# GpSimd's two-input work on VectorE and ScalarE, and the prompt's probability-value products by pairs of heads

## The chip, the cores and the metric

One Trainium2 chip, and one of its cores: TensorE (PE, with its weight loads shown apart as PEld), VectorE (DVE), ScalarE (ACT), GpSimd (POOL) and the queue engine SP, which issues most of the loads. The metric is the time of one execution on the device in microseconds (us). Before the change three runs gave a median of 1501.34 us (1498.47 to 1504.32).

## The reference

One step of a two-layer decoder over a prompt of 512 rows and a sample group of 8 sequences of 8 rows. In each layer a normalised input goes through one projection, whose columns feed a pooling mixer, a state-space mixer (causal convolution, SiLU, scan in chunks of 128) and multi-head latent attention; the three results go through an output projection and a residual add, and an MLP with a squared ReLU follows. Cut to what the change touches:

```python
def mixer(h, p, pos0, pool_hist, conv_hist, ssm_h0, attend):
    u, z, xbc, dt_raw, cq, ckv, kpe = split_in_proj(h @ p['w_in'])
    pool_out, new_pool = pool_mix(u, pool_hist, pos, p['pool_w'], p['pool_scale'])
    ssd_out, new_conv, new_ssm = ssd_mix(z, xbc, dt_raw, conv_hist, ssm_h0, p)
    mla_out, ckv_n, kpe_r = mla_mix(cq, ckv, kpe, pos, p, attend)
    y = jnp.concatenate([pool_out, ssd_out.astype(h.dtype), mla_out], axis=-1) @ p['w_out']

# ssd_mix: the convolution's output and the gate z go through SiLU
    xbc, new_conv = causal_dwconv(xbc, conv_hist, p['conv_w'], p['conv_b'])
    xbc = jax.nn.silu(xbc.astype(jnp.float32))

# mla_prompt_attn, for each block of 128 queries, all 6 heads
        sc = jnp.where(kpos[None, :] <= qpos[:, None], sc, -jnp.inf)
        pr = jax.nn.softmax(sc, axis=-1).astype(ckv.dtype)
        return jnp.einsum('bhts,bsc->bthc', pr, ckv)
```

## The kernel before

The rows are cut into two chunks: chunk 0 holds 256 rows of the prompt, chunk 1 the other 256 and the 64 sample rows. Activations lie with features on the partitions and rows along the free axis. Every large product is made from two roundings of each operand, a high and a low part: `wblock` (L183) loads half a weight block of 128 x 512 (`wr`), ACT makes its high part `wh` (L191), and the low part `wl = wr - wh` is a subtraction of two SBUF operands (L192). L192 goes to DVE for the MLP's weights and for the second half of each block of the other projections, and to POOL for the first half and for `w_uq`. `gemm` (L196) then issues three matmuls a k-tile (L201 to L203).

In a layer, `mixer` runs for each chunk: `w_in` (L502) goes through 14 column tiles, and `evac` (L460) takes each result from PSUM. The tiles named xb go through `conv_tile` (L387): two or three DVE steps bring them into `XB`, POOL copies three old columns to its front (L391), DVE makes four taps (L400, L402), ACT a sigmoid (L413 to L415), and POOL the product with it (L405, L407). There is one buffer for `XB`. The z tiles get the same sigmoid and a product on POOL (L479). The tiles cq0 and cq1 become `qhl`, from which `mla_proj` (L522) makes the queries `qT`.

`prompt_attn` (L558) goes through pairs of heads j, the two heads hh of a pair, and two blocks of 128 queries b. With `nb` blocks of 128 keys (1 or 2 in chunk 0, 3 or 4 in chunk 1) it makes scores (L570 to L574), their maximum (DVE, L576), exponentials with a sum (ACT, L579), a reciprocal (DVE, L580), the scaling by it (POOL, L581), `nb` transposes (L584), their copy `pT` to SBUF (L587 on ACT, L589 on DVE) and `nb` products with the values (L591), which write 64 partitions of PSUM: head hh = 0 the lower, hh = 1 the upper half. An fp32 product shows as two matmul records. `sample_attn` (L597) does the same for the samples from paged keys and values; POOL takes part in it at L671 and L698. `pr` and `pT` have two buffers each, shared by both.

What runs side by side is set by `Weave` (L272): generators of instructions that are taken in turn by what they have spent. The products of the MLP (`ffn`, L995) fill the time beside attention and scan. A scheduler of the compiler then sets the final order of each engine's instructions; on the chip each engine takes its own in that order.

## Time and profile before

| | us |
|---|---|
| median of three runs | 1501.34 |
| the profiled execution's own time | 1500.04 |
| its span in the profile | 1498.2 |
| PE busy | 1418.7 (95%) |
| DVE busy | 1067.8 (71%) |
| ACT busy | 816.9 (55%) |
| POOL busy | 341.5 (23%) |

The profiled execution lies 1.8 us above its span and 1.3 us under the median. Engines work beside each other, so the shares don't add up. PE shows the largest share, but matmuls are pipelined and their records overlap; how long a product holds PE is read from the distance of one start to the next.

### The profile page before, as it was taken

The page shows a single profiled execution, that of the slowest core. Times are in us where ns is not written, and L with a number is a line of the kernel's source. Part 1 is how long each engine was busy: PE and PEld are TensorE (multiplying, and loading weights), DVE is VectorE, ACT ScalarE, POOL GpSimd, SP SyncE. Part 2 cuts the span into 40 slices and gives each one's busy share as a digit, 9 for nine tenths or more (in the row PEclk, how much of TensorE's full clock was granted, in tenths as well). Part 3 has the DMA queues.
Part 4 walks back from the last instruction along what each step waited for, and adds up shares of the span by engine and source line. Part 5 has one row for each costly group of instructions (what it writes and reads, how often), then busy time and mean ns, then how long its engine had stood idle before and what let it go on. Part 6 is the DMA issues. An engine that isn't in the chain of part 4 may idle for free.

```text
span 1498.2 us, 30372 instructions
## 1 busy us (share of the span) xinstructions
PE 1418.7 (95%) x10528; PEld 1355.6 (90%) x10528; DVE 1067.8 (71%) x2225; ACT 816.9 (55%) x1717; POOL 341.5 (23%) x458
## 2 busy tenths in 40 slices
PE   5988988999999979999999999999999999999997
PEld 4867977998999978999999998889989999999997
DVE  7878759776666779865566668976866667765765
ACT  6555636555565656655454556545656565443444
POOL 5456424222200235200100035511231011000000
PEclk8999999999999999999999999989999999999999
DMA  6322425667546634434554543455675455444443
GB/s 215 108 96 77 146 70 172 201 201 211 154 138 186 199 106 135 149 104 149 163 153 153 168 153 111 149 169 165 197 225 158 135 174 165 152 150 149 149 152 108
DMA packets 151995, 228.96 MB, mean 153 GB/s; under 512 B 17826, under 2 KB 60962, under 8 KB 151714
## 3 DMA queue, kind: packets, MB, share of 16 engines
q1 hardware_dynamic: 138178, 216.69, 46.3%
q10 hardware_dynamic: 13664, 10.34, 2.3%
q8 instruction: 83, 1.36, 0.4%
q14 instruction: 70, 0.57, 0.1%
HBM read 219.32 MB, written 7.64 MB: 151 GB/s over the span
## 4 chain that ended last, share of the span: by engine, by line
PE 81%; DVE 11%; issue 2%; DMA 2%; ACT 2%; SPq 1%; POOL 0%; ACTq 0%; DVEq 0%; POOLq 0%
PE dn L203 9%; PE dn L201 9%; PE dn L202 9%; PE up L203 9%; PE up L201 9%; PE up L202 9%; PE in L203 2%; PE in L202 2%; PE in L201 2%; PE out L201 2%; PE out L202 2%; PE out L203 2%; PE o L591 2%; DVE cv L402 2%; PE spo L717 1%
## 5 line engine op out<-in xcount | busy, mean ns | idle before, releaser
L201 PE MATMUL up<-gh_f,wh_up 128*128 128x256 f32 (+1 forms) x1024 | 308.7, 302 | 5.0 <-DVE UE L425 2.6
L203 PE MATMUL up<-gh_f,wl_up 128*128 128x256 f32 (+1 forms) x1024 | 307.2, 301 | 3.4 <-DVE wl_up L192 1.9
L202 PE MATMUL up<-gl_f,wh_up 128*128 128x256 f32 (+1 forms) x1024 | 306.9, 300 | 0.7 <-DVE gl_f L236 0.5
L201 PE MATMUL dn<-hh,wh_dn 128*128 128x256 f32 (+1 forms) x1024 | 303.8, 297 | 3.3 <-ACT wh_dn L191 3.2
L203 PE MATMUL dn<-hh,wl_dn 128*128 128x256 f32 (+1 forms) x1024 | 304.2, 297 | 0.0
L202 PE MATMUL dn<-hl,wh_dn 128*128 128x256 f32 (+1 forms) x1024 | 303.3, 297 | 0.0
L191 ACT ACTIVATE wh_dn<-wr_dn 128x512 fp32r<-128x512 f32 x256 | 160.9, 631 | 184.6 <-PE dn L202 126.1
L191 ACT ACTIVATE wh_up<-wr_up 128x512 fp32r<-128x512 f32 x256 | 160.3, 630 | 172.4 <-PE up L202 107.4
L192 DVE TENSOR_TENSOR wl_dn<-wr_dn,wh_dn 128x512 fp32r<-128x512 f32 x256 | 179.2, 701 | 84.1 <-ACT wh_dn L191 72.6
L192 DVE TENSOR_TENSOR wl_up<-wr_up,wh_up 128x512 fp32r<-128x512 f32 x256 | 182.2, 715 | 73.6 <-ACT wh_up L191 63.3
L201 PEld LDWEIGHTS up<-gh_f,wh_up 128*128 128x128 f32 x1024 | 195.4, 191 | 9.0 <-DVE UE L425 2.8
L203 PEld LDWEIGHTS up<-gh_f,wl_up 128*128 128x128 f32 x1024 | 195.2, 191 | 6.8 <-DVE wl_up L192 4.6
L202 PEld LDWEIGHTS up<-gl_f,wh_up 128*128 128x128 f32 x1024 | 195.7, 191 | 2.6 <-DVE gl_f L236 0.8
L201 PEld LDWEIGHTS dn<-hh,wh_dn 128*128 128x128 f32 x1024 | 193.3, 189 | 3.9 <-ACT wh_dn L191 3.7
L203 PEld LDWEIGHTS dn<-hh,wl_dn 128*128 128x128 f32 x1024 | 193.2, 189 | 1.4 <-issue 0.7
L202 PEld LDWEIGHTS dn<-hl,wh_dn 128*128 128x128 f32 x1024 | 193.3, 189 | 1.2 <-issue 0.9
L201 PE MATMUL in<-gh_h,wh_in 128*128 128x256 f32 (+3 forms) x448 | 137.9, 308 | 16.2 <-DVE cq L490 7.5
L203 PE MATMUL in<-gh_h,wl_in 128*128 128x256 f32 (+3 forms) x448 | 137.6, 307 | 3.5 <-DVE wl_in L192 2.4
L202 PE MATMUL in<-gl_h,wh_in 128*128 128x256 f32 (+3 forms) x448 | 137.2, 306 | 2.1 <-DVE gl_h L236 2.1
L192 POOL TENSOR_TENSOR wl_in<-wr_in,wh_in 128x512 fp32r<-128x512 f32 (+1 forms) x55 | 72.9, 1326 | 155.8 <-ACT wh_in L191 149.8
L192 POOL TENSOR_TENSOR wl_out<-wr_out,wh_out 128x512 fp32r<-128x512 f32 x32 | 41.8, 1306 | 278.7 <-ACT wh_out L191 278.7
L201 PEld LDWEIGHTS in<-gh_h,wh_in 128*128 128x128 f32 (+1 forms) x448 | 85.1, 190 | 18.9 <-issue 7.9
(349 smaller groups left out, 2849.4 us busy)
## 6 DMA issues: line engine op xcount, KB each, us to landing
wr_up<-in_w_up SPq DMA_DIRECT2D x256, 256.0 KB, 2.8
wr_dn<-in_w_down SPq DMA_DIRECT2D x256, 256.0 KB, 2.8
wr_in<-in_w_in SPq DMA_DIRECT2D x110, 256.0 KB, 2.8
wr_out<-in_w_out SPq DMA_DIRECT2D x64, 256.0 KB, 2.9
ku<-in_kcache SPq DMA_DIRECT2D x96, 128.0 KB, 2.9
nat<-in_ncache SPq DMA_DIRECT2D x96, 64.0 KB, 2.0
ku<-in_kcache ACTq DMA_DIRECT2D x32, 128.0 KB, 3.7
wr_uq<-in_w_uq SPq DMA_DIRECT2D x12, 256.0 KB, 2.8
```

Source lines behind the costliest of these rows:

```text
L191: A.activation(hh, r, AF.Copy)
L192: (V if eng == 'v' or (f and eng is None) else G).tensor_tensor(ll, r, hh.bitcast(F32), op=ALU.subtract)
L201: T.matmul(ps[:mw, :cw], wh[:, kk, :mw], ah, start=(k == 0), stop=False)
L202: T.matmul(ps[:mw, :cw], wh[:, kk, :mw], al, start=False, stop=False)
L203: T.matmul(ps[:mw, :cw], wl[:, kk, :mw], ah, start=False, stop=(k == nk - 1))
L402: V.scalar_tensor_tensor(cv[:, :n], X[:, k:k + n], par(l, 'conv_w', m * 4 + k), cv[:, :n], op0=ALU.mult, op1=ALU.add)
L591: mark_pe[f"pa{l}{c}"] = T.matmul(po[64 * hh:64 * hh + 64, b * P:b * P + P], vT[i // 2][:, i % 2, h * 64:h * 64 + 64], pT[:, i * P:i * P + ...
L717: mark_pe[f"s{l}{2 * pq_ + 1}"] = T.matmul(po[:, 64 * u:64 * u + NR], nat[:, g], pT[:, o_:o_ + NR], start=False, stop=True, skip_group_che ...
```

## The change

Four things, all in the code that is shown above.

- The tables of engines at L93: the products with the sigmoids (L405, L407, L479) and the correction of the rotary keys of the cache (L671) go from POOL to DVE.
- `wblock`: all subtractions L192 go to DVE.
- The scalings by the reciprocal, L581 in the prompt and L698 in the samples, become ACT activations with a scale of one value a partition.
- `prompt_attn`: the loops over heads and query blocks change places. For one query block the steps up to `pT` are made for both heads of a pair; then their products stand in turns, one of head 0, one of head 1. `pT` is copied by ACT for the second head and by DVE for the first, where it was by query block. The yields keep their sum, 1.1 nb a pair.

POOL keeps the memsets, the small copies, the squares at the start (L247 to L251), the pooling sums (L436), L886, L890 and two products at the end (L1021).

```diff
-    E_XA, E_Z, E_KR, E_PR = G, G, G, G
+    E_XA, E_Z, E_KR = V, V, V
...
-                (V if eng == 'v' or (f and eng is None) else G).tensor_tensor(ll, r, hh.bitcast(F32), op=ALU.subtract)
+                V.tensor_tensor(ll, r, hh.bitcast(F32), op=ALU.subtract)
...
                 po = psum('ac', f"o{l}{c}{j}")
-                for hh in range(2):
-                    h = 2 * j + hh
-                    for b in range(2):
-                        nb = 2 * c + b + 1
-                        nk = nb * P
+                for b in range(2):
+                    nb = 2 * c + b + 1
+                    nk = nb * P
+                    pTs = []
+                    for hh in range(2):
+                        h = 2 * j + hh
...
-                        E_PR.tensor_scalar(pr[:, :nk], pr[:, :nk], nm[:, 3:4], 1.0, op0=ALU.mult, op1=ALU.mult)
+                        A.activation(pr[:, :nk], pr[:, :nk], AF.Copy, scale=nm[:, 3:4])
...
-                        if b:
+                        if hh:
                             A.activation(pT[:, :nk], tp[:, :nk], AF.Copy)
                         else:
                             V.tensor_copy(pT[:, :nk], tp[:, :nk])
-                        for i in range(nb):
+                        pTs.append(pT)
+                        yield 0.4 * nb
+                    for i in range(nb):
+                        for hh in range(2):
+                            h = 2 * j + hh
                             mark_pe[f"pa{l}{c}"] = T.matmul(
                                 po[64 * hh:64 * hh + 64, b * P:b * P + P], vT[i // 2][:, i % 2, h * 64:h * 64 + 64],
-                                pT[:, i * P:i * P + P], start=(i == 0), stop=(i == nb - 1)).ins
-                        yield 0.55 * nb
+                                pTs[hh][:, i * P:i * P + P], start=(i == 0), stop=(i == nb - 1)).ins
+                    yield 0.3 * nb
...
-                G.tensor_scalar(prs[1], prs[1], nm[:, 1:2], 1.0, op0=ALU.mult, op1=ALU.mult)
+                A.activation(prs[1], prs[1], AF.Copy, scale=nm[:, 1:2])
```

The scheduler makes a new order of all engines from this. Five lines more in the file move the line numbers: L591 of before is L596 after.

On PE, in layer 0, chunk 1, the products of heads 4 and 5 with the first query block (`pT0140` is `pT` of layer 0, chunk 1, head 4, query block 0; `vT00` and `vT01` are the values of the chunks). Before:

```order
L202 MATMUL up0024_5980<-gl_f00_3370,wh_up0024_0_5970 128x256
L591 MATMUL o012_6101<-pT0140_6117,vT00_906 64x128 x2
L591 MATMUL o012_6101<-pT0140_6117,vT01_3498 64x128
L570 MATMUL sc0151_6678<-kT00_905,qT01_3074 128x256
L571 MATMUL sc0151_6678<-kT01_3497,qT01_3074 128x256
```

After:

```order
L733 MATMUL spv01_6294<-ol01_3756,uv0_200 64x64
L596 MATMUL o012_6101<-pT0140_6117,vT00_906 64x128
L596 MATMUL o012_6101<-pT0150_6247,vT00_906 64x128
L596 MATMUL o012_6101<-pT0140_6117,vT00_906 64x128
L596 MATMUL o012_6101<-pT0150_6247,vT00_906 64x128
L596 MATMUL o012_6101<-pT0140_6117,vT01_3498 64x128
L596 MATMUL o012_6101<-pT0150_6247,vT01_3498 64x128
L585 MATMUL pt0151_6647<-cst_77,pr0151_6643 128x128 x4
```

The three products of head 5 stood in a burst of their own 36 rows further on and now stand between those of head 4. Not all bursts are so clean: in most the scheduler puts the first product of one head ahead, alone, and the others follow in turns.

On DVE, shortly after the start (`r_q00` is the factor of the queries, `qT00` the queries of layer 0, chunk 0, `gl_h0_1` the low part of chunk 1's input, `sm00` small steps of the scan). Before:

```order
L236 SCALAR_TENSOR_TENSOR gl_h0_1_155<-x1_in_152,prm0_73,gh_h0_1_154 128x320
L499 SCALAR_TENSOR_TENSOR r_q00_306<-tab00_214,r_q00_306 128x256
L786 SCALAR_TENSOR_TENSOR sm00_435<-sm00_435 128x18
L192 TENSOR_TENSOR wl_in004_4_644<-wr_in004_4_641,wh_in004_4_643 128x512
L531 TENSOR_TENSOR qT00_590<-q000_597,r_q00_306 128x256
L531 TENSOR_TENSOR qT00_590<-q001_605,r_q00_306 128x256
```

After:

```order
L481 TENSOR_TENSOR ckvn00_217<-in001_483,r_in00_211 128x256
L499 SCALAR_TENSOR_TENSOR r_q00_306<-tab00_214,r_q00_306 128x256
L779 TENSOR_TENSOR sm00_435<-dt00_432,prm0_73 128x12
L531 TENSOR_TENSOR qT00_590<-q000_597,r_q00_306 128x256
L782 SCALAR_TENSOR_TENSOR sm00_435<-sm00_435 128x18
L531 TENSOR_TENSOR qT00_590<-q001_605,r_q00_306 128x256
L531 TENSOR_TENSOR qT00_590<-q002_619,r_q00_306 128x256
L531 TENSOR_TENSOR qT00_590<-q003_627,r_q00_306 128x256
L784 TENSOR_SCALAR sm00_435<-sm00_435 128x18
L793 TENSOR_SCALAR sm00_435<-sm00_435 128x18
L236 SCALAR_TENSOR_TENSOR gl_h0_1_155<-x1_in_152,prm0_73,gh_h0_1_154 128x320
```

The row of L236 in the first piece is the last of eight; all eight now stand behind `r_q` and four of the `qT`. On ACT the two steps of `r_q` (L217, L218) stood around chunk 1's high parts (L235) and now stand together, ahead of the two `kT` copies (L537, L538) and of L235.

On DVE, from one xb tile of chunk 1 to the next (`XB011` is tile 1; `wl_out` belongs to the output projection of chunk 0). Before:

```order
L390 TENSOR_TENSOR XB011_2164<-in017_2139,r_in01_1897 128x256
L394 TENSOR_TENSOR XB011_2164<-in017_2139,r_in01_1897 128x8x8
L400 TENSOR_SCALAR cv011_2171<-XB011_2164,prm0_73 128x344
L402 SCALAR_TENSOR_TENSOR cv011_2171<-XB011_2164,prm0_73,cv011_2171 128x344 x2
L745 SCALAR_TENSOR_TENSOR o00_1175<-o00_1175,prm0_73,r_o00_2282 128x256 x3
L402 SCALAR_TENSOR_TENSOR cv011_2171<-XB011_2164,prm0_73,cv011_2171 128x344
L192 TENSOR_TENSOR wl_out000_4_2348<-wr_out000_4_2345,wh_out000_4_2347 128x512
```

After:

```order
L390 TENSOR_TENSOR XB011_2177<-in017_2152,r_in01_1910 128x256
L394 TENSOR_TENSOR XB011_2177<-in017_2152,r_in01_1910 128x8x8
L192 TENSOR_TENSOR wl_out000_0_2342<-wr_out000_0_2339,wh_out000_0_2341 128x512
L400 TENSOR_SCALAR cv011_2184<-XB011_2177,prm0_73 128x344
L750 SCALAR_TENSOR_TENSOR o00_1175<-o00_1175,prm0_73,r_o00_2282 128x256 x3
L402 SCALAR_TENSOR_TENSOR cv011_2184<-XB011_2177,prm0_73,cv011_2184 128x344
L405 TENSOR_TENSOR xaz01_1915<-cv010_2111,se010_2116 128x256
L407 TENSOR_TENSOR xaz01_1915<-cv010_2111,se010_2116 128x64
```

A subtraction and the two products of the tile before have come in between the taps.

## Rows read from the trace of the kernel before

**Rows 1.** The page: shares of the span in the chain that ended last, by engine.

```profile
PE 81%; DVE 11%; issue 2%; DMA 2%; ACT 2%; SPq 1%; POOL 0%; ACTq 0%; DVEq 0%; POOLq 0%
```

**Rows 2.** Busy time by stretch: us, PE, PEld, DVE, ACT, POOL, granted clock, DMA, GB/s.

```profile
545.00:610.00 65.00, 58.37 (x443) 54.71 (x444) 55.92 (x126) 41.11 (x96) 29.29 (x40) 0.96 0.37 115
...
880.00:985.00 105.00, 97.66 (x755) 87.38 (x755) 88.44 (x188) 57.81 (x130) 54.41 (x79) 0.98 0.41 130
```

**Rows 3.** PE's waits: whom for, us in total, times, the longest.

```profile
PE q L201 <- DVE qT L531: 13.9, 2, 12.2
```

**Rows 4.** PE by line and form: count, busy us, mean ns; then bursts in time: start, us.

```profile
L591 PE MATMUL o<-pT,vT 128*64 128x128 f32 x240 | 35.3, 283 | 1.5 <-ACT pT L587 1.5
```

```profile
262.39 0.87 PE L591 MATMUL o<-pT,vT 128*64 128x128 f32 x6
263.19 0.38 PE L203 MATMUL up<-gh_f,wl_up 128*128 128x256 f32 x1
...
288.10 1.09 PE L591 MATMUL o<-pT,vT 128*64 128x128 f32 x8
289.12 0.39 PE L202 MATMUL dn<-hl,wh_dn 128*128 128x256 f32 x1
```

**Rows 5.** PE in time: products of the scan, whose heads stand in turns.

```profile
599.37 0.88 PE L871 MATMUL y<-rm,xd 128*64 128x128 f32 x12
600.07 0.49 PE L904 MATMUL st<-xe,bt 128*64 128x192 f32 x4
```

**Rows 6.** The start in time: DVE, then ACT, then PE.

```profile
36.64 0.54 DVE L236 SCALAR_TENSOR_TENSOR gl_h<-x_in,prm,gh_h 128x320 fp32r<-128x320 f32 x1
37.10 0.41 DVE L499 SCALAR_TENSOR_TENSOR r_q<-tab,r_q 128x256 f32<-128x256 f32 x1
```

```profile
26.62 0.47 ACT L217 ACTIVATE r_q<-ss_q,eps 128x256 f32<-128x256 f32 x1
...
31.74 0.41 ACT L218 ACTIVATE r_q<-r_q 128x256 f32<-128x256 f32 x1
```

```profile
42.82 0.38 PE L201 MATMUL in<-gh_h,wh_in 128*128 128x256 f32 x1
```

**Rows 7.** POOL by line and form: count, busy us, mean ns, idle before and releaser.

```profile
L192 POOL TENSOR_TENSOR wl_in<-wr_in,wh_in 128x512 fp32r<-128x512 f32 x51 | 69.3, 1359 | 149.7 <-ACT wh_in L191 143.6 <-DVE cq L490 2.3 <-DVE ah L807 2.1
L671 POOL TENSOR_TENSOR kh<-ku,kh 32x256 fp32r<-32x256 f32 x64 | 56.5, 886 | 162.7 <-ACT kh L669 121.1 <-issue 24.6 <-DMA wr_up<-in_w_up 11.4
L192 POOL TENSOR_TENSOR wl_out<-wr_out,wh_out 128x512 fp32r<-128x512 f32 x32 | 41.8, 1306 | 278.7 <-ACT wh_out L191 278.7
...
L581 POOL TENSOR_SCALAR pr<-pr,nm 128x512 f32<-128x512 f32 x12 | 8.8, 737 | 42.3 <-DVE nm L580 32.9 <-DVE qll L631 4.9 <-DMA nat<-in_ncache 4.5
```

**Rows 8.** DVE by line and form, and two lines' shortest, median and longest ns.

```profile
L670 DVE TENSOR_TENSOR kl<-ku,kh 128x256 fp32r<-128x256 f32 x64 | 38.5, 602 | 18.2 <-ACT kh L669 16.9 <-DMA ku<-in_kcache 1.1
...
L402 DVE SCALAR_TENSOR_TENSOR cv<-XB,prm,cv 128x344 f32<-128x344 f32 x30 | 24.3, 809 | 0.6
...
L402 DVE SCALAR_TENSOR_TENSOR cv<-XB,prm,cv 128x256 f32<-128x256 f32 x30 | 22.3, 742 | 0.6
```

```profile
L402 DVE SCALAR_TENSOR_TENSOR cv<-XB,prm,cv x60: 466/577/1651, 49.6 to 930.7; 128x256 f32<-128x256 f32 x30, 128x344 f32<-128x344 f32 x30
```

**Rows 9.** Chunk 1's xb tiles in time: DVE, then POOL.

```profile
128.91 1.50 DVE L402 SCALAR_TENSOR_TENSOR cv<-XB,prm,cv 128x344 f32<-128x344 f32 x1
...
131.78 0.68 DVE L192 TENSOR_TENSOR wl_in<-wr_in,wh_in 128x512 fp32r<-128x512 f32 x1
132.38 0.33 DVE L412 TENSOR_SCALAR cv<-cv 128x344 f32<-128x344 f32 x1
132.63 0.41 DVE L390 TENSOR_TENSOR XB<-in,r_in 128x256 f32<-128x256 f32 x1
```

```profile
128.36 1.67 POOL L192 TENSOR_TENSOR wl_in<-wr_in,wh_in 128x512 fp32r<-128x512 f32 x1 [0.33 <-ACT wh_in L191]
```

**Rows 10.** ACT by line and form: exponentials over 512 columns.

```profile
L579 ACT ACTIVATE pr<-sc,nm 128x512 f32<-128x512 f32 x12 | 8.2, 686 | 13.1 <-DVE nm L577 9.1 <-PE pt L584 3.2 <-PE spo L717 0.7
```

## The prediction

> **What bounds the kernel now.** I read the chain of work that ended last first: 81% of it lies on PE and 11% on DVE, 0% on POOL [rows 1]. So POOL's own time is worth nothing by itself; the change can pay only by shortening work on PE, by ending a wait of PE, or by what POOL does to DVE. Then the stretches: in layer 1's input projections (545 to 610 and 880 to 985 us) DVE is busy 55.92 of 65 and 88.44 of 105 us, 86% and 84%, and there PE stands idle for 6.6 and 7.3 us [rows 2]; nearly all the rest is covered by MLP products. Then PE's waits: one of 12.2 us at the start, for a `qT` of DVE, is the longest by far [rows 3]. Last, the products that the change reorders, one by one in time [rows 4, 5]. The sum is made against the profiled execution, 1500.04 us, which lies 1.3 under the median of the three runs.
>
> **The value products (A).** There are 240 records of L591 [rows 4]. In a burst of one head the next instruction starts 0.80 us after the first of six records (262.39 to 263.19) and 1.02 us after the first of eight (288.10 to 289.12) [rows 4]: 0.11 us a record and 0.14 fixed a burst. The trace has them in 45 bursts, so they hold PE for 240 x 0.11 + 45 x 0.14 = 32.7 us. What two heads in turns would cost is seen in the scan, whose products L871 have the same form, 128 rows on 64 columns over 128, and alternate between the lower and the upper 64 partitions: there the next instruction starts 0.70 us after the first of twelve records (599.37 to 600.07) [rows 5], where one after the other would take 12 x 0.11 + 0.14 = 1.46. Two in turns run at once. In the changed order I counted, burst by burst, the products of the head that has more of them: 79 of the 120, since a lone product often goes ahead. That is 158 records one after another in 43 bursts: 158 x 0.11 + 43 x 0.14 = 23.4. **A = -9.3 us.** The ends are 0, if they don't overlap here, and -13.2, half of all records, if no product stood alone. Nearly all of it lies beside the MLP, where no other engine ends a wait of PE's, so it should reach the end of the span; only chunk 0 of layer 0 (four products saved, under 1 us) lies where PE waits anyway.
>
> The Trainium skill has a rule that speaks against this: "TensorE: Matmul & The Clock Gate", Part 3, under what overlaps and what doesn't, says that a weight load overlaps a running matmul only where its row group is another. Both heads here use all 128 rows, so by that rule A would be about 0 and the sum some nine us higher. The scan's row, with the same row groups, shows twelve records in 0.70 us, and I go by it.
>
> **The start (B).** Before, PE's wait of 12.2 us [rows 3] stands here, for the queries' factor `r_q`: ACT made its first step at 26.62 and the second only at 31.74, behind eight high parts of chunk 1, and DVE used it at 37.10, behind eight low parts of chunk 1, the last of which started at 36.64 and took 0.54 [rows 6]. In the changed order both ACT steps stand ahead of these, and on DVE `r_q` and four `qT` do. PE then has the next projection tile to do, and that is late next: its low weights, which POOL made early, now stand on DVE behind the same eight low parts, ready at 37.18 + 0.60 = 37.8 if nothing else moves (0.60 is a subtraction's pitch on DVE, 131.78 to 132.38 [rows 9]). Before, that tile began at 42.82 [rows 6]. **B = -5.0 us**, with -8 (part of DVE's work before it also gets shorter) and 0 (DVE's chain behind it gives all back) as ends.
>
> **DVE's load (C).** Added: 100 subtractions (51 for `w_in`, 32 for `w_out` [rows 7], 12 for `w_uq` and five of other forms) at 0.60 are 60 us; 64 corrections of the rotary keys and 32 products over 256 or 320 columns at 0.41 (a 256-column step [rows 9]) 39; ten small ones some 2. Together 101 us on an engine that is busy 1067.8. Taken off: while POOL runs, DVE's steps on SBUF operands stretch. A tap L402 took 1.50 us at 128.91, while a POOL subtraction ran from 128.36 for 1.67 [rows 9]; the median of this line is 0.577 and its forms' means are 0.809 and 0.742 [rows 8], some 12 us too much over 60. The 64 `kl` steps take 0.602 [rows 8] where 0.41 would do, 12 us. So where POOL meets such a step, its subtraction already costs DVE 0.92; done by DVE itself it costs 0.60. Where it meets none it costs DVE nothing before and 0.60 after. With DVE busy 85% of the time in the projections, and about half of its work of the sensitive kind, that is 0.85 x 0.5 x 0.92 = 0.39 before against 0.60 after: +0.2 us for each of the 68 subtractions of `w_in` and `w_uq`, 14 us of DVE time in about 290 us of projections. Against it stands what is shorter on the way to PE: a subtraction takes 0.68 instead of 1.36 [rows 7, 9], and the products and POOL's small copies no longer stand in one queue with it. **I take C = 0.** The ends: -14, the 14 us that PE idles in layer 1's two projections; and +21, if each of the 20 xb tiles becomes longer by what DVE gets, a subtraction and its products, 0.60 + 0.41 + 0.05, and nothing comes back.
>
> **ACT and the buffers (D).** 48 scalings of the prompt and 8 of the samples move to ACT. POOL took 0.737 for 512 columns [rows 7]; the nearest row of ACT is an exponential of the same size with 0.686 [rows 10]. At most 56 x 0.69 = 39 us come onto an engine that is busy 55%, mostly beside MLP products. As a step between scores and transposes it gets no longer, so without that cover it still costs nothing: D = 0. `pT` changes engines without a change in amount. A new wait: the products of a pair wait for both heads' `pT`, and both buffers stay taken until then, so a sample group's copy on ACT can stand behind them, and weights' high parts behind that. MLP products hide it; without them it is one more step of about 0.69 for each of 24 pairs and blocks, 17 us.
>
> **The sum:** 1500.04 - 9.3 - 5.0 = 1485.7, told as **1486**.
>
> **Rivals.**
> *More comes back.* With a shorter way from weights to PE, and no 1.5 us steps in DVE's chain, PE's idle time in the projections goes. 12 of the 14 us of layer 1 would give 1474. For it: the stretched rows [rows 8, 9]. Against it: DVE does more work in the same stretches.
> *The pairs don't overlap* and the products cost what they did, but for two bursts less (0.3): 1500.04 - 5.0 - 0.3 = 1495, no change that a measurement shows. For it: these products add up in one place over several key blocks, which the scan's twelve do not. Against it: the scan's row. This is what that rule of the Trainium skill would make of it.
> *DVE gives part back.* A and B hold, and half of the upper end of C is paid: 1486 + 10 = 1496, again no change.
> *DVE becomes the bound, slower than before.* In each xb tile DVE's taps, subtractions and products stand in one line with one `XB` buffer. If its load there, 86% now, goes to all of the time, each tile's DVE work sets the pace: C = +21, and the start's gain is given back, since DVE is what the tiles behind it wait for: 1500.04 - 9.3 + 21 = 1512. It decides from the point at which the added 1.06 us a tile is more than the idle time DVE has left, (65 - 55.92)/14 = 0.65 us a tile, plus what the collisions give back. Against it: one tap in three has only to lose its 0.92.
>
> **How the numbers follow.** The forecast has 0.42, more comes back 0.22, no overlap 0.13, part given back 0.13, slower 0.10. The forecast's own range is 1480 to 1492. The range must leave out no more than 0.2: from 1470 to 1502 it leaves out the slower case and some 0.06 under 1470. About 0.5%, 7.5 us, is what a measurement of this kernel can tell from no change: under 1493.8 is faster, over 1508.8 slower. The first two cases are faster, with a little off the forecast's upper end and a little back from the two cases near 1495: 0.66. No change 0.25, slower 0.09.
>
> **What would show it.** A: the value products' bursts, six records of two heads in about 0.47 us from first to next instead of 0.80, and their neighbours unmoved. B: no wait of PE over 10 us for `qT`; the third pair of query products before 30 us; the first xb tile on PE near 38. C: POOL busy about 82 us; L402 near its 0.577 in the mean; DVE busy between 1080 and 1150 us; PE's idle time in the projections no longer than now. D: no wait of PE for a `pT` over 1 us in the middle of MLP work. I would be wrong if PE's waits for DVE grow in the projections by more than 14 us, or if the scheduler's order, which was made anew everywhere, puts PE behind a load or a copy at places that I have not looked at; one wait like that at the start shows how much a place can cost.

## The result

The changed kernel takes 1463.72 us in the median, the kernel before on the same chip 1499.9: a ratio of 0.9753 (95% interval 0.9729 to 0.9778), 36 us faster. The forecast was 1486, its range ended at 1470: the sign was right, and the size that was forecast less than half of this. The execution that was profiled with these runs was a disturbed one of 6642.7 us, as was one run of 4725.64 us of the one-input kernel below, so all rows of the changed kernel here come from two more profiled executions of the same kernel, 1462.5 and 1458.5 us long; where nothing else is said, from the first.

The page of the changed kernel, busy time by engine and the chain that ended last by engine (before: [rows 1], and the table ahead):

```profile
PE 1408.9 (96%) x10528; PEld 1345.9 (92%) x10528; DVE 1079.1 (74%) x2431; ACT 843.6 (58%) x1773; POOL 83.7 (6%) x196
PE 88%; DVE 7%; ACT 2%; DMA 1%; issue 1%; SPq 0%; DVEq 0%; POOL 0%; ACTq 0%
```

By the prediction's count DVE got some 101 us more to do, and it is busy for 11 more. DVE's share of the chain fell from 11% to 7%.

Busy time in the two stretches of [rows 2], shifted by what the kernel had gained there, so that they start at the same products and end near them; columns as there:

```profile
526.70:585.90 59.20, 56.49 (x427) 53.44 (x427) 52.17 (x136) 38.98 (x88) 4.61 (x15) 0.94 0.41 127
859.20:954.80 95.60, 95.59 (x711) 87.28 (x709) 86.50 (x216) 59.55 (x133) 22.14 (x45) 0.97 0.43 138
```

PE idles for 2.7 and 0.0 us here, 6.6 and 7.3 before, though DVE's share rose to 88% and 90%. So a fuller DVE did not hold PE up more. Of the 7.3 us before, 3.5 are two waits of PE for loads of a scan state, which come back below.

PE's longest waits (before: the 12.2 us of [rows 3] stood on top):

```profile
PE in L201 <- DVE cq L490: 7.9, 1, 7.9
PE in L201 <- ACT wh_in L191: 5.1, 1, 5.1
PE in L201 <- ACT gh_h L235: 4.9, 1, 4.9
PE up L202 <- DVE gl_f L961: 3.8, 3, 3.0
```

The start in time, ACT, then DVE, then PE (before: [rows 6]; x2 and x4 are rows run together):

```profile
23.21 0.47 ACT L217 ACTIVATE r_q<-ss_q,eps 128x256 f32<-128x256 f32 x1
23.80 0.42 ACT L218 ACTIVATE r_q<-r_q 128x256 f32<-128x256 f32 x1
...
30.22 1.90 ACT L235 ACTIVATE gh_h<-x_in,prm 128x320 fp32r<-128x320 f32 x4
32.03 1.13 ACT L191 ACTIVATE wh_in<-wr_in 128x512 fp32r<-128x512 f32 x2
```

```profile
24.35 0.41 DVE L499 SCALAR_TENSOR_TENSOR r_q<-tab,r_q 128x256 f32<-128x256 f32 x1
25.35 0.42 DVE L531 TENSOR_TENSOR qT<-q,r_q 128x256 f32<-128x256 f32 x1 [0.43 <-PE q L203]
...
35.03 1.00 DVE L236 SCALAR_TENSOR_TENSOR gl_h<-x_in,prm,gh_h 128x320 fp32r<-128x320 f32 x2
36.05 1.28 DVE L192 TENSOR_TENSOR wl_in<-wr_in,wh_in 128x512 fp32r<-128x512 f32 x2
```

```profile
32.69 0.58 PE L201 MATMUL in<-gh_h,wh_in 128*128 128x256 f32 x1 [5.11 <-ACT wh_in L191]
...
36.78 0.58 PE L203 MATMUL in<-gh_h,wl_in 128*128 128x256 f32 x1 [2.25 <-DVE wl_in L192]
```

The two ACT steps of `r_q` stand together, `qT` follows its products at once, and the wait for it is gone. Its heir is the next tile, behind chunk 1's preparation on both engines: its high part is late on ACT, its low part on DVE.

The value products on PE: the group, then two bursts with what came next (before: [rows 4]):

```profile
L596 PE MATMUL o<-pT,vT 128*64 128x128 f32 x240 | 27.3, 290 | 0.8 <-DVE nm L578 0.8
```

```profile
91.80 0.65 PE L596 MATMUL o<-pT,vT 128*64 128x128 f32 x6
92.38 0.48 PE L865 MATMUL cb<-xaz 64*128 64x128 f32 x2
...
311.56 1.09 PE L596 MATMUL o<-pT,vT 128*64 128x128 f32 x14
312.58 0.39 PE L679 MATMUL ssc<-kl,qlh 128*128 128x256 f32 x1
```

Six records of two heads take 0.58 us from first to next, where six of one head took 0.80; fourteen take 1.02, as eight of one head did. The six are three products, two of one head and one of the other, since a first product went ahead alone: by the prediction's own prices 4 x 0.11 + 0.14 = 0.58, and 8 x 0.11 + 0.14 = 1.02 for the fourteen. Its 0.47 had taken half of the six records.

DVE's steps that POOL used to stretch, and its subtractions now (before: [rows 8], and 0.60 to 0.68 in [rows 9]):

```profile
L675 DVE TENSOR_TENSOR kl<-ku,kh 128x256 fp32r<-128x256 f32 x64 | 26.9, 421 | 16.8 <-ACT kh L674 16.2
...
L402 DVE SCALAR_TENSOR_TENSOR cv<-XB,prm,cv 128x344 f32<-128x344 f32 x30 | 17.1, 570 | 0.2
...
L402 DVE SCALAR_TENSOR_TENSOR cv<-XB,prm,cv 128x256 f32<-128x256 f32 x30 | 14.3, 477 | 0.1
```

The taps went from 809 and 742 ns to 570 and 477, the `kl` steps from 602 to 421. Over all groups of DVE that have as many steps after as before, the durations add up to some 87 us less. Set against the shortest duration of each group, all of DVE's steps together are 134 us too long before and 51 in the changed kernel.

Where the time went, by starts of the same product (us from the span's start; the marks are the first product of L201 in chunk 1's first input tile of layer 0, behind the 14 tiles of chunk 0, in the output projections of the four chunks in their order, and in the last MLP block). The other columns are kernels of the next section:

| first product of | before | changed | changed, again | moves alone | pairs alone | subtractions alone | products alone |
|---|---|---|---|---|---|---|---|
| first input tile, layer 0 chunk 1 | 85.66 | 80.28 | 80.60 | 80.64 | 90.38 | 79.88 | 88.19 |
| output, layer 0 chunk 0 | 140.47 | 130.88 | 130.32 | 130.54 | 142.46 | 128.58 | 138.65 |
| output, layer 0 chunk 1 | 481.78 | 463.01 | 463.61 | 474.34 | 476.95 | 469.16 | 478.44 |
| output, layer 1 chunk 0 | 707.76 | 686.97 | 687.34 | 698.53 | 703.87 | 692.23 | 704.64 |
| output, layer 1 chunk 1 | 1196.95 | 1161.95 | 1157.93 | 1175.21 | 1186.85 | 1175.85 | 1183.89 |
| last MLP block | 1459.23 | 1423.43 | 1419.42 | 1435.45 | 1449.11 | 1436.09 | 1444.59 |

Two executions of the changed kernel part by 4 us between two of these marks, so a difference of one profile under some 4 us says nothing by itself. The first mark of the column before is an early one: the kernels in which PE's long wait for `qT` stands as before (pairs, products, scalings and keys alone) pass it at 87.4 to 90.4.

PE's part in these stretches, each up to its mark, and how long PE is idle in it (us):

| stretch up to | before | idle | changed | idle | moves alone | idle |
|---|---|---|---|---|---|---|
| first input tile, layer 0 chunk 1 | 85.7 | 21.5 | 80.3 | 14.6 | 80.6 | 15.3 |
| output, layer 0 chunk 0 | 54.8 | 9.8 | 50.6 | 6.6 | 49.9 | 6.4 |
| output, layer 0 chunk 1 | 341.3 | 14.9 | 332.1 | 10.0 | 343.8 | 13.8 |
| output, layer 1 chunk 0 | 226.0 | 12.3 | 224.0 | 9.2 | 224.2 | 8.6 |
| output, layer 1 chunk 1 | 489.2 | 9.9 | 475.0 | 1.7 | 476.7 | 0.2 |
| last MLP block | 262.3 | 1.9 | 261.5 | 2.0 | 260.2 | 1.6 |

Up to the last mark PE is busy for 1389.0 us before, 1389.6 with the moves alone and 1379.3 in the changed kernel, and idle for 70.2, 45.8 and 44.2. By these profiles the moves shorten what PE waits, and the pairs what it works.

The granted clock of PE has a part in it that these runs don't separate. In the kernel before and the changed one it is at 0.50, the 1.2 GHz level, in stretches of 3 to 14 us: between layer 1's two output projections the first profile of the changed kernel has 6.8 us of it, the second none, and they part by 4.4 us there. The mean granted clock of the runs of one group is 0.978 before, 0.981 in the changed kernel and 0.982 with the moves alone. Were PE the limit throughout, that would be 5 to 6 us of their gains, by (1 - clock) times the run's time; it is an estimate.

### The profile page after: what moved, and what is told of

Same layout as the page of the kernel before. It is cut to its first block, busy times and chain, and to the rows that moved or that the text cites. A ratio compares the mean times of both kernels' runs of the same rounds, so it can differ in the third digit from the quotient of the medians.

```text
span 6642.7 us, 30130 instructions
## 1 busy us (share of the span) xinstructions
PE 6616.1 (100%) x10528; PEld 6082.8 (92%) x10528; DVE 1084.4 (16%) x2431; ACT 868.9 (13%) x1773; POOL 71.4 (1%) x196
## 4 chain that ended last, share of the span: by engine, by line
PE 100%; DVE 0%; ACT 0%; DMA 0%; issue 0%; DVEq 0%; ACTq 0%
PE up L203 10%; PE up L201 10%; PE up L202 10%; PE dn L201 9%; PE dn L203 9%; PE dn L202 9%; PE in L203 5%; PE in L201 5%; PE in L202 5%; PE out L201 3%; PE out L202 3%; PE out L203 3%; PE spo L722 2%; PE o L596 1%; PE rb L852 1%; PE pt L585 1%
## 5 line engine op out<-in xcount | busy, mean ns | idle before, releaser
L201 PE MATMUL up<-gh_f,wh_up 128*128 128x256 f32 (+1 forms) x1024 | 985.9, 964 | 0.7 <-ACT gh_f L235 0.7
L203 PE MATMUL up<-gh_f,wl_up 128*128 128x256 f32 (+1 forms) x1024 | 983.3, 962 | 0.0
L202 PE MATMUL up<-gl_f,wh_up 128*128 128x256 f32 (+1 forms) x1024 | 975.9, 954 | 0.0
L203 PE MATMUL dn<-hh,wl_dn 128*128 128x256 f32 (+1 forms) x1024 | 958.9, 937 | 0.0
L201 PE MATMUL dn<-hh,wh_dn 128*128 128x256 f32 (+1 forms) x1024 | 958.4, 936 | 0.0
L202 PE MATMUL dn<-hl,wh_dn 128*128 128x256 f32 (+1 forms) x1024 | 954.9, 933 | 0.0
L201 PEld LDWEIGHTS up<-gh_f,wh_up 128*128 128x128 f32 x1024 | 765.1, 747 | 41.7 <-issue 24.2
L203 PEld LDWEIGHTS up<-gh_f,wl_up 128*128 128x128 f32 x1024 | 759.0, 741 | 45.9 <-issue 29.3
L202 PEld LDWEIGHTS up<-gl_f,wh_up 128*128 128x128 f32 x1024 | 762.3, 745 | 31.6 <-issue 15.0
L201 PEld LDWEIGHTS dn<-hh,wh_dn 128*128 128x128 f32 x1024 | 744.3, 727 | 30.7 <-issue 17.2
L201 PE MATMUL in<-gh_h,wh_in 128*128 128x256 f32 (+3 forms) x448 | 510.8, 1141 | 12.1 <-DVE cq L490 7.1
L201 PEld LDWEIGHTS in<-gh_h,wh_in 128*128 128x128 f32 (+1 forms) x448 | 402.0, 897 | 33.0 <-issue 26.1
L203 PEld LDWEIGHTS in<-gh_h,wl_in 128*128 128x128 f32 (+1 forms) x448 | 398.0, 888 | 27.7 <-issue 22.2
L202 PEld LDWEIGHTS in<-gl_h,wh_in 128*128 128x128 f32 (+1 forms) x448 | 402.1, 898 | 17.7 <-issue 17.3
L192 DVE TENSOR_TENSOR wl_up<-wr_up,wh_up 128x512 fp32r<-128x512 f32 x256 | 176.2, 689 | 975.5 <-ACT wh_up L191 725.5
L192 DVE TENSOR_TENSOR wl_dn<-wr_dn,wh_dn 128x512 fp32r<-128x512 f32 x256 | 176.0, 688 | 815.6 <-ACT wh_dn L191 580.4
```

The source lines that it names most:

```text
L192: V.tensor_tensor(ll, r, hh.bitcast(F32), op=ALU.subtract)
L201: T.matmul(ps[:mw, :cw], wh[:, kk, :mw], ah, start=(k == 0), stop=False)
L202: T.matmul(ps[:mw, :cw], wh[:, kk, :mw], al, start=False, stop=False)
L203: T.matmul(ps[:mw, :cw], wl[:, kk, :mw], ah, start=False, stop=(k == nk - 1))
```

## Experiments: the two halves of the change, and the pairs taken apart

The theory now: A and B as forecast, C missed. The rivals: the pairs are worth more than forecast, or the gain is an accident of the new order.

**The changed kernel again** (no edit).

> The changed kernel itself, for a trace. All theories: 36 us faster than before (ratio 0.975, about 1464 us). The prediction's rows: PE's 12.2 us wait for qT gone, POOL busy near 82 us, six value products from first to next in about 0.47 us if two heads run at once and in about 0.80 us if they don't.

Measured 1464.41 us against 1497.9, ratio 0.977 (0.9737 to 0.9804); its rows stand above. POOL is busy for 83.7 us. The burst of six took 0.58, between the two expected numbers, since the six records are not three pairs.

**The pairs alone.** The changed kernel with

```diff
-    E_XA, E_Z, E_KR = V, V, V
+    E_XA, E_Z, E_KR = G, G, G
...
-                V.tensor_tensor(ll, r, hh.bitcast(F32), op=ALU.subtract)
+                (V if eng == 'v' or (f and eng is None) else G).tensor_tensor(ll, r, hh.bitcast(F32), op=ALU.subtract)
```

and the two scalings back on POOL.

> Only the new loop order of the prompt's attention, products of two heads in turns and pT copied by head; all work of GpSimd stays where it was. Theory 1 (the prediction's sizes of A, and C was missed): 9 us faster than before, 1491. Theory 2 (the pairing is worth more than it was given): 20 us faster or more, 1480 or less. Theory 3 (the gain comes from the new order of the whole, not from the parts): some 0 to 5 faster.

1489.09 us, 8.8 less than before, ratio 0.9943 (0.9922 to 0.9965): theory 1. Its PE waits 12.7 us for `qT` as before, and the table's column shows no gain at the start and gains of 6.8 and 6.2 us in the stretches with chunk 1's attention.

**The moves alone.** The kernel before with the same engines as the changed one, and its own loops.

> Only the work of GpSimd moves, all of it as in the change; the prompt's attention keeps its loop order. Theory 1: 27 us faster than before, 1473, of which 5 at the start. Theory 2: at most 16 us faster, 1484. Theory 3: 0 to 10 faster, and the two parts together fall short of 36 by more than 15.

1475.37 us, 22.5 less, ratio 0.9841 (0.9801 to 0.9881). The halves add up to 31.3 of some 34 to 36; theory 3 falls, and theory 2 too, but theory 1's 27 is missed by 4.5. In the table, 5.0 us are won up to chunk 1's first input tile, 4.9 more up to the first output projection, 2.5 lost in layer 0's chunk 1, and 1.8 and 12.5 won in layer 1.

**Head after head.** The changed kernel with

```diff
-                    for i in range(nb):
-                        for hh in range(2):
+                    for hh in range(2):
+                        for i in range(nb):
```

> The changed kernel, but the value products of a pair stand head after head instead of in turns. If two heads in turns run at once: 9 us slower than the changed kernel, 1473. If they don't overlap: no difference from it, 1464, within 2 us.

1473.99 us, ratio 0.9839 (0.9806 to 0.9871): 9.6 more than the changed kernel in the same group. The products take turns at PE for a gain. Added up from first to next, the bursts hold PE for 32.7 us before, 24.2 in the changed kernel and 29.6 here: head after head, they still overlap a little where one head hands over to the other (16 records in 1.51 us).

```profile
427.73 1.58 PE L596 MATMUL o<-pT,vT 128*64 128x128 f32 x16
429.24 0.39 PE L201 MATMUL up<-gh_f,wh_up 128*128 128x256 f32 x1
```

So 5.4 of the 9.6 us lie in the bursts. By the profiles the rest is not the overlap: 8.4 us are lost in the stretch of layer 0's chunk 1 alone, where the bursts hold PE for 2.3 us longer, and the scheduler's order is another one here too.

## Experiments: the moves one by one

Each is the kernel before with one group of steps moved. **The subtractions** (L192 on `V` throughout):

> The kernel before, with nothing but all low parts of weights (L192) on VectorE. Theory S (GpSimd's work stretches VectorE's steps, and these steps are what PE waits for): the subtractions are about half of the 258 us that left GpSimd, and nearly all of its work in the projections: 12 to 16 of the 22.5 us of the moves, 1482 to 1486. Theory L (a slow GpSimd subtraction is itself late for PE): 18 or more, 1480 or less. Theory O (the order at the start alone, 10 us, the rest chance): 10 if the start's order changes as in the changed kernel, else 0.

1478.21 us against 1496.51, 18.3 less, ratio 0.9879 (0.9859 to 0.9899): the number of L (18 or more) and above S's 12 to 16. It has the whole gain of the start (11.9 us at the first output projection).

**The products** (`E_XA, E_Z, E_KR, E_PR = V, V, V, G`):

> The kernel before, with nothing but the products with the sigmoids and the correction of the rotary keys on VectorE. Theory S: these are 34 us of GpSimd in the projections and 57 beside the MLP, where no step of VectorE ends a wait of PE: 3 to 6 us faster, 1492 to 1495. Theory L: nothing, within 3 us of 1498. Theory O: nothing, or whatever the start's order gives.

1488.71 us, 7.8 less, ratio 0.9941 (0.9915 to 0.9967). The size is above S's, and the place is not S's as I had put it: 9.9 us are won in layer 1's second half, between its two output projections, where I had said no step of DVE ends a wait of PE. The profiled execution is 13.7 us shorter than the one before, though the medians part by 7.8, so its places are rough.

**The scalings** (L581 and L698 on ACT):

> The kernel before, with nothing but the scalings of the probabilities on ScalarE. All theories: 0 to 3 us faster, 1495 to 1498. More would say that the scaling stands on the way to PE in chunk 0's attention.

1492.97 us, 3.5 less, ratio 0.9977 (0.9964 to 0.9989), a little above the expected end; the mean granted clock, 0.9819 against 0.9805, can be 2 of them by the estimate above.

**The rotary keys alone** (`E_XA, E_Z, E_KR, E_PR = G, G, V, G`), later, in another group:

> The kernel before, with the correction of the rotary keys alone on VectorE (of the three groups of products moved together before, which gave 8 us, of them 10 between the two output projections of layer 1). If the stretched steps around the sample attention and the scan of the states are what cost there: 4 to 8 us faster than before, nearly all in layer 1's second half. If it was the products with the sigmoids: within 2 us of the kernel before.

1492.03 us against 1499.01, 7.0 less, ratio 0.9965 (0.9942 to 0.9987); 4.5 us of it in layer 1's second half. That is hardly more than what two executions part by, so a share of the keys there is likely, not shown.

One by one the three groups give 18.3 + 7.8 + 3.5 = 29.6 us, together 22.5. With intervals of 3 to 6 us each it can't be said how much of the same waits they share.

What happens in layer 1's second half, in the kernel before: DVE, then POOL, then SP's load of a scan state, then PE and a window of 10 us (columns as in [rows 2]).

```profile
971.06 0.17 DVE L580 RECIPROCAL nm<-nm 128x1 f32<-128x1 f32 x1
971.14 2.56 DVE L1014 TENSOR_TENSOR hl<-fr,hh 128x256 fp32r<-128x256 f32 x1
973.73 0.61 DVE L618 TENSOR_TENSOR qs<-qs,qT 32x384 f32<-32x384 f32 x1
974.37 0.56 DVE L894 TENSOR_TENSOR h<-h,sst 128x384 f32<-128x384 f32 x1
```

```profile
969.12 2.14 POOL L890 TENSOR_SCALAR bm<-bt,cst 64x128 f32<-64x128 f32 x2 [2.47 <-PE sst L892]
971.23 0.82 POOL L886 TENSOR_TENSOR h<-h,tot 128x384 f32<-128x384 f32 x1
972.04 0.58 POOL L581 TENSOR_SCALAR pr<-pr,nm 128x384 f32<-128x384 f32 x1
972.59 0.82 POOL L886 TENSOR_TENSOR h<-h,tot 128x384 f32<-128x384 f32 x1
973.40 1.18 POOL L890 TENSOR_SCALAR bm<-bt,cst 64x128 f32<-64x128 f32 x2
```

```profile
979.27 0.33 SPq L878 DMA_DIRECT2D h<-in_state_ssm  x1
```

```profile
981.76 1.45 PE L883 MATMUL y<-Ez,h 128*64 128x8 f32 x24 [2.45 <-DMA h<-in_state_ssm]
```

```profile
981.00:991.00 10.00, 8.21 (x74) 7.38 (x75) 4.36 (x11) 1.84 (x4) 1.66 (x2) 0.50 0.54 179
```

A step `hl` of the MLP, which takes 0.41 us just before (at 969.23), takes 2.56 beside POOL's steps, back to back. Behind it in DVE's queue stands the state's update L894; its result is stored, its buffer is loaded anew at 979.27, and PE waits 2.45 us for that load, and 1.03 at 984.24 for the next one. The granted clock of PE is 0.50 from 981 to 991, the 1.2 GHz level. This chain is read from the order of the rows and was not tried by itself; none of the POOL steps in it shows in the page's chain. The Trainium skill, "SBUF — State Buffer", section "SBUF: two separate sides", says of VectorE's steps with two SBUF inputs and GpSimd's steps that read SBUF that whichever starts first holds a shared port for its whole instruction and the other blocks. The row of 2.56 us agrees: it starts while a POOL step runs and lasts over three more (971.23 to 973.41). That it let several pass in turn is more than that section says.

## Experiments: GpSimd's load put back

In these the changed kernel keeps everything, and POOL makes extra steps for weights' blocks into a buffer that nobody reads. The edit, in `wblock` behind L192, in one line, with the blocks that were POOL's own:

```diff
+    [G.tensor_tensor(junk[:, :w_, :mw], hh[:, s:s + w_].bitcast(F32), hh[:, s:s + w_].bitcast(F32), op=ALU.subtract) for s, w_ in ((0, 1), (1, 1), (2, 1), (3, 1)) if not (eng == 'v' or (f and eng is None))]
```

> The changed kernel, and beside it GpSimd makes subtractions of the size that it made before (four of 128 columns for each of the blocks that were its own) into a buffer that nobody reads; nobody waits for it and the order on the other engines is nearly the same. Theory S: the steps on VectorE get longer again (the tap L402 back from 524 to 650 ns or more in the mean) and the kernel is 8 us or more slower than the changed one, 1472 or more. Theory L: no more than 3 us slower, 1467. Theory O: the start is the same, so no difference but chance, within 3 us.

1482.06 us, ratio 0.9905 (0.9883 to 0.9928); its profiled execution is 17.7 us longer than the changed kernel's. More than half of what the moves gave is gone, though DVE waits for POOL hardly longer (4.5 us in all, 3.7 in the changed kernel, 18.8 in the kernel before). The taps got longer, but less than expected (524 to 573 ns over both forms), and DVE's durations by 37.6 us in all. **Half of it**, `((0, 1), (2, 1))`:

> As the kernel with four subtractions of GpSimd beside each block, but with two. Theory S: half the work, half the loss, 7 to 11 us slower than the changed kernel, 1471 to 1475. If the loss came from a place where the order changed, not from the load: anything between 0 and 18.

1475.66 us, ratio 0.9831 (0.9791 to 0.9872), a little above S's 1475. **One input** in place of two, `G.tensor_copy(junk..., hh...)`:

> The changed kernel, and beside it GpSimd makes four copies of 128 columns (one input) for each of the blocks that were its own, into a buffer that nobody reads. If it is the second input of GpSimd's steps that holds VectorE up: no more than 3 us slower than the changed kernel, 1467. If any work of GpSimd on SBUF does it, or if it is GpSimd's queue, behind which its small copies and sums are late: slower by as much for each us of GpSimd as the four subtractions cost (18 us for 243 us of them), some 8 to 15 us, 1472 to 1479.

1474.71 us, ratio 0.9835 (0.9793 to 0.9876), though DVE's durations grew by 10.5 us only. These three don't tell the theories apart as I had meant: the scheduler made other orders around chunk 0's attention for them, and from chunk 1's first input tile to its third all three are 3.2 to 3.6 us longer than the changed kernel (33.1 to 33.5 us against 29.87), whatever their load. **Beside the MLP**, `if eng == 'v' and not f and name[:2] == 'dn'`, which leaves the order of all other engines as it was:

> The changed kernel, and beside it four such subtractions of GpSimd for every other block of the MLP's second weights, 128 blocks, more than 300 us of GpSimd; the order on every other engine is word for word that of the changed kernel. If a stretched VectorE costs only where PE waits for it: VectorE's steps beside the MLP get longer, by 30 us or more in all, and the time stays within 4 us, 1468. If it costs everywhere: 18 us or more, 1482.

1468.89 us, ratio 0.9796 (0.9762 to 0.9829). The extra POOL row, and the MLP's subtractions on DVE, which take 690 ns in the changed kernel:

```profile
L192 POOL TENSOR_TENSOR junk<-wh_dn 128x128 bf16<-128x128 f32 x512 | 310.6, 607 | 681.6 <-ACT wh_dn L191 646.9 <-ACT fr L1014 3.1
```

```profile
L192 DVE TENSOR_TENSOR wl_dn<-wr_dn,wh_dn 128x512 fp32r<-128x512 f32 x256 | 187.3, 734 | 82.0 <-ACT wh_dn L191 74.2 <-PE dn L203 1.9 <-PE dn L201 0.8
```

310 us of POOL lengthen DVE by 29.5 us and the kernel by some 4, which is within what two executions part by. In the projections about as much stretching costs 8.3 us (below); that it costs less where PE does not wait for DVE is likely by this, not clearly told.

**The load in the unchanged order.** To take the order out, the blocks were chosen so that PE's and DVE's order is word for word the changed kernel's (those of layer 0's chunk 1 and of `w_uq` are left out, since the order changes with them): `if not f and (name[:3] in ('in1', 'out') or name[:4] == 'in00')`, with the four subtractions, and with scalings, one input in place of two.

> The changed kernel, and beside it four subtractions of 128 columns of GpSimd for the first half of each weight block of layer 0's first, of layer 1's two input projections and of the output projections: 296 of them, some 180 us, read by nobody. The order of TensorE and VectorE is word for word that of the changed kernel, so no chance of another order is in it. Theory S (GpSimd's load lengthens VectorE's steps on the way to PE): 8 to 14 us slower than the changed kernel on the same chip. If the losses before came from other orders: within 3 us of it.

> The same, with one input in place of two: a scaling of the same 128 columns at the same places, as many instructions, in the same order on TensorE and VectorE. If it is the second input that holds VectorE up: within 3 us of the changed kernel. If any load of GpSimd does, or GpSimd's queue: as much as the subtractions, in proportion to the time that these take on GpSimd.

> The changed kernel once more, on the chip of the others of this group, as what they are compared with: 0.975 to 0.977 of the kernel before; and its trace against the first one's, which tells how far two executions of one order lie apart at the same places (2 us or less).

On one chip, six runs each: the changed kernel 1463.69 us (1460.25 to 1467.21), with subtractions 1471.95 (1467.41 to 1475.01), with scalings 1465.33 (1462.39 to 1467.95); ratios to before 0.9777 (0.9748 to 0.9806), 0.982 (0.9791 to 0.9849), 0.9783 (0.9754 to 0.9812). The two traces of the changed kernel part by 4.4 us between two marks, where 2 or less was expected. The extra steps of POOL and the taps on DVE, first with two inputs, then with one:

```profile
L192 POOL TENSOR_TENSOR junk<-wh_in 128x128 bf16<-128x128 f32 x156 | 96.6, 619 | 166.5 <-ACT wh_in L191 156.0 <-ACT tot L824 1.8 <-POOL XB L391 0.2
...
L192 POOL TENSOR_TENSOR junk<-wh_out 128x128 bf16<-128x128 f32 x128 | 79.4, 621 | 655.3 <-ACT wh_out L191 642.1 <-ACT fr L1014 5.8
```

```profile
L402 DVE SCALAR_TENSOR_TENSOR cv<-XB,prm,cv 128x344 f32<-128x344 f32 x30 | 18.4, 613 | 0.2
```

```profile
L192 POOL TENSOR_SCALAR junk<-wh_in 128x128 bf16<-128x128 f32 x156 | 79.8, 511 | 180.4 <-ACT wh_in L191 169.2 <-ACT tot L824 2.4
...
L192 POOL TENSOR_SCALAR junk<-wh_out 128x128 bf16<-128x128 f32 x128 | 62.8, 490 | 669.1 <-ACT wh_out L191 661.2
```

```profile
L402 DVE SCALAR_TENSOR_TENSOR cv<-XB,prm,cv 128x344 f32<-128x344 f32 x30 | 17.3, 576 | 0.2
```

180 us of two-input work on POOL lengthen DVE's durations by 27.7 us and the kernel by 8.3, with no run of the one kernel among those of the other; 146 us with one input lengthen DVE by 10.5 and the kernel by 1.6, which is not told from nothing. The mean granted clocks, 0.9815 and 0.9822, leave some 1 us of the 8.3 to the clock. So S is shown, in the order that the changed kernel has: GpSimd's two-input work costs time by making DVE's steps longer; one-input steps at the same places, of 146 us, don't cost what 180 us of two-input ones do. GpSimd's queue as it was before is not put back by this: DVE waits for POOL 3.7 us in the changed kernel and 3.9 and 4.2 here, but 18.8 in the kernel before, 11.3 of them the state's update L894 for POOL's product L886, and 3.8 with the subtractions alone moved. What those waits cost is untried. How much of the 22.5 us it is stays an estimate: the moved work was some 260 us, and 8.3 x 260/180 = 12.

## Experiments: a faster version

**The rest of POOL's two-input work moved too**: in the changed kernel the pooling sums (L436), the scan states' products (L891) and two last products (L1026) on DVE, the products with the sequence masks (L895) on ACT.

> The changed kernel, with the rest of GpSimd's two-input work moved too: the pooling sums, the products of the scan's states and of the last output to VectorE, the 16 products with the sequence masks to ScalarE; only the squares at the start and the small copies stay. Theory S: 2 to 6 us faster than the changed kernel, 1458 to 1462. If VectorE's load counts by now: 2 to 5 slower.

1461.4 us, ratio 0.9749 (0.9716 to 0.9782): not told from the changed kernel. **Chunk 1's preparation later**, on top of that:

```diff
-        tc.cur_priority = at + 400
+        tc.cur_priority = at + 800
```

> A version to beat both kernels: the changed kernel, with the rest of GpSimd's two-input work moved as well and chunk 1's preparation 400 places later in the scheduler's order (800 in place of 400). In the changed kernel TensorE waits 5.4 us at 27 us for a high part that stands on ScalarE behind eight of chunk 1's, and 2.7 at 34 for a low part behind eight on VectorE. If the preparation is hidden later: 4 to 8 us faster than the changed kernel, 1456 to 1460. If it only moves into the xb tiles, where VectorE is the fuller engine: no faster, 1462 or more.

> The same with 200 places (600 in place of 400), so that chunk 1's preparation comes just behind the tile that waits. If it is hidden there: 3 to 7 us faster than the changed kernel, 1457 to 1461. If it only moves: no faster, 1462 or more.

1458.63 us, 0.9743 (0.9721 to 0.9764), with 800, and 1461.46, 0.9753 (0.9731 to 0.9775), with 600. The first is the fastest kernel of this study, by an amount that its interval doesn't separate from the changed kernel. The marks tell why: with 800 the fifth and seventh input tiles start 4.3 and 11.6 us earlier than in the changed kernel (28.42 and 36.27 against 32.73 and 47.91), chunk 1's first 3.8 later (84.36 against 80.60), and the first output projection 1.7 earlier (128.64 against 130.32). The wait at the start was hardly a cost of its own; DVE and ACT have that work to do before chunk 0's attention anyway. What did change is the clock: with 800 the profile has no stretch at 0.50 before 72 us, where the changed kernel's second one has 10.2 us from 31.6, which begin in PE's wait of 5.1 us up to 32.73, and the runs' mean is 0.988 against 0.982. By the estimate above that is 8 us, more than the whole gain.

## Why the prediction was right in two terms and wrong in the third

- **A, the value products: right.** Forecast -9.3; -8.8 alone, and 9.6 lost when they stand head after head, of which the bursts are 5.4. The bursts went from 32.7 to 24.2 us where 23.4 was forecast, and PE's busy time fell by some 10. The scan's row [rows 5] was the right guide, and the rival that they don't overlap fell. What "TensorE: Matmul & The Clock Gate" of the Trainium skill says in Part 3, that loads overlap only across row groups, did not hold for these 64-column halves: fourteen records of two heads in 1.02 us.
- **B, the start: right.** Forecast -5.0, measured -5.4 and -5.1 at chunk 1's first input tile; against the other kernels that keep the old start it would be -7 to -10, so the close hit is in part luck. The step inside it held as well: the heir of the wait is the tile's low part behind eight low parts of chunk 1, forecast ready at 37.8, used at 36.78. That the tile's high part would be late on ACT too, for 5.1 us, was not forecast.
- **C, DVE's load: the step that failed.** It was taken as 0, with -14 as its end; the moves gave -22.5, of which B is 5, so C was some -17 (in part the clock's, as said above). Two things were wrong in its sum. First its bookkeeping of DVE: I let about 27 us of collisions go (0.39 for each of 68 subtractions) and named some 24 in two groups of steps, where some 87 went, against 101 added. The forecast of DVE busy, 1080 to 1150, shows it: 1079.1 came out. Second what DVE's steps are worth to PE: what DVE gets was set against a shorter way to PE without a price, and the balance was called 0. PE's idle time shows the price: 70.2 us before, 45.8 with the moves alone, of which the stretch of the start is 6.3. In layer 1 13.4 us of idle time went, about the 14 that were named as the end; 4.5 more went in layer 0, of which the end had nothing. The two waits for scan states, 3.5 us, which stand behind a stretched step of DVE in the rows, are among the 14. POOL's 0% in the chain [rows 1] was read as "its own time is worth nothing"; its effect was in the rows of DVE, and what part of it was DVE's 18.8 us of waiting for POOL is open.
- **More comes back**, the rival that came nearest, had the mechanism right and its price at 12 us, the idle time again. **DVE becomes the bound** fell: DVE is fuller in the projections and PE waits less.
- **D, ACT and the buffers:** no loss; the scalings alone gave 3.5, some 2 of them perhaps the clock's, where 0 was taken.
- **The range** ended at 1470, C's lower end with little beyond. An end for a cost that the trace shows only in part (one row of 1.50 us, one median) should have come from all of DVE's groups set against their shortest durations, 134 us in the kernel before, not from the waits that I could see.

Not settled: how the other 5 us or so of C divide between POOL's queue, the new order and the clock, why the three groups alone sum to 7 us more than together, and why the whole gives 2 to 5 us more than its two halves.

## What to carry to other kernels

Where GpSimd and VectorE run beside each other, set every VectorE line's mean against its shortest duration: the excess is the most that GpSimd can cost there (134 us here before, and 51 were left with GpSimd busy for 6% of the span), and what of it counts is paid where TensorE waits behind VectorE's queue, in whatever stage that is. A step on GpSimd that costs nothing in the chain may cost a neighbour's queue. To test such a load by itself, put it back where the order of the other engines stays the same word for word; with another order, a difference of a few us is not the load's.

## What the runs showed that I had not expected

- GpSimd's steps with two inputs lengthened VectorE's by 27.7 us for 180 us, those with one input by 10.5 for 146: per us, 0.15 against 0.07.
- A VectorE step of 0.41 us took 2.56 beside GpSimd's steps in a row; it let several of them pass, not one.
- Products of two heads that write different halves of 64 columns seem to run at once even where one head follows the other as a whole, at the place where they change: 16 records in 1.51 us, where 16 x 0.11 + 0.14 = 1.90 was to be expected. The bursts of 8 and 12 records with such a change save the same four records (0.59 and 1.03 to 1.07).
